# Head loads of a hybrid attention block: [hi; lo] keys, plain rows on SyncE's queue, 13 slots, five raw weight buffers

## The chip, the cores and the metric

One core of one Trainium2 chip runs the kernel. The metric is the device time of one execution in microseconds (us), as the median of several. The engines are TensorE (PE; its weight loads are listed as PEld), VectorE (DVE), ScalarE (ACT), GpSimd (POOL) and SyncE (SP). DMAs are issued by SyncE's and GpSimd's queues, each in its own order.

## The reference

One layer of a decoder over 1024 tokens of width 1024, in float32: a normalised input is projected once for three token mixers, their outputs are projected back and added, and a squared-ReLU MLP with a hidden width of 4096 follows.

```python
h = rms_norm(x, norm_mix[l])
proj = h @ w_in[l]
a_q, a_kv, a_g, b_qkv, c_qkv = jnp.split(proj, PROJ_SPLITS, axis=-1)
o_a = nsa_mixer(...)             # 4 heads: compressed, selected and window attention, gated
o_b = dilated_mixer(...)         # 3 groups (dilation 1, 4, 16) of 2 heads, merged by denominators
o_c = stick_breaking_mixer(...)  # 6 heads: sigmoid scores, running products from the right
cat = jnp.concatenate([...], axis=-1)
x = x + cat @ w_out[l]
h = rms_norm(x, norm_mlp[l])
x = x + jnp.square(jax.nn.relu(h @ w_up[l])) @ w_down[l]
```

Heads have 64 columns. All attention is causal, in blocks of 128 queries.

## The kernel before

Every float32 operand of a matmul is split into two float32r halves, hi (a rounded copy, on ScalarE) and lo (what is left, on VectorE or GpSimd); `put` (L107) does both. A dense product is three matmuls (hi·hi, hi·lo, lo·hi) that add up in one PSUM bank.

The tokens are two halves of 512. Queries and keys of the stick-breaking and dilated heads are projected pair by pair (two heads are 128 columns), split, and spilled to DRAM tensors `q_d`, `k_d` (`spill_qk`, L538): for each pair one store of the hi tile and one of the lo tile, each with 128 rows, the two heads' 64 columns one below the other. Values go to `v_d` with hi and lo side by side in the free dimension (`spill_v`). NSA queries of the second half go to `nq_d` in the same way (L443); those of the first half stay in SBUF.

A unit of attention work loads its heads with `load_heads` (L597). A key tile has the 64 hi rows above the 64 lo rows of one head. The query tiles `qh` and `ql` have the hi rows twice and the lo rows twice, so the two matmuls of `scores` (L632) give hi·hi + hi·lo and lo·hi + lo·lo. All these loads are issued by GpSimd: for a pair two of qh, two of ql, two of k, two of v; for a single head two of q, one of k, one of v; for NSA four. The q loads read their source rows twice, and the k loads step over the two stored parts with an outer dimension. v is read as it lies.

The tiles of these loads come from one pool of 11 slots of 128 x 1024 (`slots`, L119). The program that writes the kernel keeps a count of live slots (`live`, `take`, `free`, `prefetch`, L1322) against `SLOTS` (L213); a unit whose slots don't fit is loaded after another one has ended. Units need: stick-breaking pair 4 slots in the first half and 6 in the second, dilated unit 6 and 9, NSA 4 for keys and values and 2 for each pair of heads' queries. Probabilities lie in the `ck` pool (10 buffers).

Units run in the order: first half stick-breaking pairs 0, 1, 2, dilated 0, 1, NSA; second half NSA, stick-breaking 0, 1, dilated 0, 1, stick-breaking 2. While one unit's probabilities are multiplied with the values, the next one's scores are made (`both`, L1351); the dilated units of the second half run alone. Between the steps of the units the program puts steps of a filler: projections, then the output projection and the MLP of the first half. After the last unit the second half's output projection and MLP run without attention. Dilated units exchange softmax statistics through DRAM (`xch`, L951 to L966, SyncE).

Weights of the input projection are loaded by SyncE into raw buffers (`wraw`, two of them, L168) in parts of 128 x 512; `split` (L176) casts and subtracts a part and then asks for the part after next. A weight group has two or four parts; the next group is fetched as soon as a group comes into use (`next_w`, L316). Split weights lie in pairs of tiles `whi`, `wlo` (three pairs). Output and MLP weights go through `load_rows` (L1042): into the same raw buffers at first, and into four of their own once the MLP's pool is open.

The order of the instructions on each engine is set when the kernel is built, from the program above and a simulated timeline; each engine then works in that order.

Of the kernel before, what the change touches and what calls it, by code (L numbers as in the profile page):

```python
# [15 lines left out]

S, D, HD, DFF = 1024, 1024, 64, 4096
NB = S // 128
EPS = 1e-6
WMAX = 268  # L20
# [39 lines left out]
def tile_trunk(ctx, tc, x, xT, w_in, w_out, w_up, w_down, cw1, cw2, small, t_nsa, t_dil, out):  # L60
# [24 lines left out]
    r_d = dram.tile([S], F32, name="r_d")  # L85
    nq_d = dram.tile([2, 2, 2, 64, 512], F32, name="nq_d")
    q_r, k_r, v_r, nq_r = [t.bitcast(F32R) for t in (q_d, k_d, v_d, nq_d)]

# [29 lines left out]
    hctx = ExitStack()  # L118
    slots = actx.enter_context(tc.tile_pool(name="slots", bufs=11))  # L119
    ckp = actx.enter_context(tc.tile_pool(name="ck", bufs=10))  # L120
    ptp = actx.enter_context(tc.tile_pool(name="pT", bufs=3))
# [19 lines left out]
    def load_w(key):  # L141


        if key[0] == 'w1':
            n, pieces, src, o0 = 128, 2, cw1[key[1]], 0
        else:
            n = len(W_GROUPS[key])
            pieces, src, o0 = 1 if n == 128 else 2, w_in, W_OFF[key]
        res, parts = [], []
        k = 8 if key[0] == 'w1' else 8 // pieces  # L150
        for i in range(pieces):
            o = o0 + i * k * n
# [12 lines left out]
        def load(part):  # L165
            dst = part[1]
            m = dst.shape[1] * (dst.shape[2] if len(dst.shape) == 3 else 1)
            raw = wpool.tile([128, 2 * WMAX], F32, tag="wraw", bufs=2, name="wraw")[:, :m]  # L168
            i = nc.sync.dma_start(raw, src[:, part[0]:part[0] + m])
            if clock[0] < 10.0:  # L170
                in_order(i)
            return raw.rearrange("p (k c) -> p k c", c=128) if len(dst.shape) == 3 else raw

        raws = [load(p) for p in parts[:2]]

        def split():  # L176
            for i, (_, hi, lo) in enumerate(parts):
                put(hi, lo, raws[i], pool=i % 2 == 1 and len(w_keys) < 14)
                if i + 2 < len(parts):
                    raws.append(load(parts[i + 2]))  # L180
                if i % 2:
                    yield
        return res, split()
# [28 lines left out]
    FLIP, START, END = 1.3, 5.0, 2.5  # L212
    SLOTS = 11  # L213
    live = [2]
# [214 lines left out]
    def nsa_q(W_q, half):  # L429
# [6 lines left out]
        def fin(p):  # L436
            tp = pair_T(v2, 128 * p)
            if half == 1:
                hi, lo = [sg_t("tnq", F32R)[:, :512] for _ in range(2)]
                for i, r in ((0, A), (1, B)):  # L440
                    put(hi[r], lo[r], tp[r], qg[r, 2 * p + i:2 * p + i + 1])
                for part, t in enumerate((hi, lo)):
                    nc.sync.dma_start(nq_d[p, part].rearrange("h d t -> (h d) t"), t.bitcast(F32))  # L443
                return
            nsa['q', 0, p] = hi, lo = [slot(n).rearrange("p (h t) -> p h t", h=2) for n in ("nqh", "nql")]
            for i, r in ((0, A), (1, B)):
                put(hi[A, i], lo[A, i], tp[r], qg[r, 2 * p + i:2 * p + i + 1])
                nc.scalar.copy(hi[B, i], hi[A, i].bitcast(F32))
                nc.vector.tensor_copy(lo[B, i], lo[A, i].bitcast(F32))
        for p in range(2):  # L450
# [85 lines left out]


    def spill_qk(pair, j, cs, hi, lo):  # L538
        for part, t in enumerate((hi, lo)):
            nc.sync.dma_start((q_d, k_d)[j][pair, part, :, cs], t.bitcast(F32))  # L540

# [50 lines left out]

    def rows_of(t, *dims):

        return bass.AP(tensor=t.tensor, offset=t.offset, ap=[list(d) for d in dims])

    def load_heads(pair, half, heads=(0, 1)):  # L597

        q0, nk = 512 * half, 512 * (half + 1)
        ks = slice(0, nk)  # L600
        n = len(heads)
        hs = slice(heads[0], heads[0] + n)
        halves = lambda t: t.rearrange("p (h s) -> p h s", h=2)
        part, twice = (128 * S, 2), (0, 2)
        if n == 1:
            r = 64 * heads[0]
# [11 lines left out]
        qh, ql = [halves(slot(nm)) for nm in ("qh", "ql")]  # L618
        k, v = [[t[:, 0], t[:, 1]] if half == 0 else [t, slot(nm)]
                for nm in "kv" for t in [halves(slot(nm)) if half == 0 else slot(nm)]]  # L620
        for i, t in enumerate((qh, ql)):
            for h in heads:
                r = 64 * h
                nc.gpsimd.dma_start(t[:, h], rows_of(q_r[pair, i, r:r + 64, q0:q0 + 512], twice, (S, 64), (1, 512)))
        for h in heads:
            r = 64 * h
            nc.gpsimd.dma_start(k[h], rows_of(k_r[pair, 0, r:r + 64, ks], part, (S, 64), (1, nk)))
        for h in heads:
            nc.gpsimd.dma_start(v[h], v_r[pair, h, :, ks])
        return [(qh[:, h], ql[:, h], k[h], v[h]) for h in heads]  # L630

    def scores(qh, ql, n, k, masked=False):  # L632

# [4 lines left out]
        cs = slice(128 * n, 128 * n + 128)  # L638
        nc.tensor.matmul(o, qh[:, cs], k, start=True, stop=False)  # L639
        if masked:  # L640
            nc.tensor.matmul(o[:, w - 128:w], ident_r, ahead, start=False, stop=False)
        nc.tensor.matmul(o, ql[:, cs], k, start=False, stop=True)  # L642
        return ps
# [101 lines left out]
    class Nsa(Unit):  # L745
# [21 lines left out]
        def branch(self, i, chunks, kt, vt, gate, l0):  # L767

            n, h = self.n, 2 * self.hp + i
            (qh, ql), sl, st = [t[:, i] for t in nsa['q', self.half, self.hp]], SLOPES[6 + h], self.st[i]  # L770
            prev = None
            for k, (p, c0, tab) in enumerate(chunks):
                w = p.shape[-1]
                acc = st[:, 4 * l0 + k:4 * l0 + k + 1]
                ps = scores(qh, ql, n % 4, kt[:, c0:c0 + w])
                biased(ps, w, tab, sl, p, acc, prev)
# [55 lines left out]
    class Sb(Unit):  # L832
# [16 lines left out]
        def weights(self, n, c0):  # L849

            qh, ql, k, _ = self.head
# [4 lines left out]
            ps = scores(qh, ql, n % 4, k[:, c0:c0 + w], masked=after is None)  # L856
            nc.scalar.activation(b[:, :w], ps[:, :w], AF.Sigmoid, scale=-0.125)
# [37 lines left out]
    class Dil(Unit):  # L895
# [18 lines left out]
        def probs(self):  # L914
# [9 lines left out]
            for ro in range(4):  # L924
# [9 lines left out]
                for g in (1, 2):  # L934
                    qh, ql, k, _ = hd[g]
                    if half == 0:
# [4 lines left out]
                    acc = acc_t[:, ro:ro + 1] if g == 1 else stP[:, ro, 0:1]  # L941
                    biased(scores(qh, ql, ro, k), w, dtab[:, 256 * g - w:256 * g], 4.0 * sl[g], p, acc, prev)
                    prev = acc
# [8 lines left out]
            nc.sync.dma_start(self.oN, dP.rearrange(nat, p=128))  # L952
            qh, ql, k, _ = hd[0]
            for i in range(4):
# [5 lines left out]
                p = pn[-1][:, 256 * (i % 2):256 * (i % 2) + w]  # L960
                ps = scores(qh, ql, i, k[:, c0:c0 + w])
                biased(ps, w, dtab[:, 256 - w:256], sl[0], p, stN[:, i, 0:1], None)
# [74 lines left out]
    def raw_tile():  # L1037
        if 'mp' in late:
            return late['mp'].tile([128, 512], F32, tag="raw", bufs=4, name="raw")
        return wpool.tile([128, 2 * WMAX], F32, tag="wraw", bufs=2, name="wraw")[:, :512]  # L1040

# [419 lines left out]
```

## Time and profile before

| | us |
|---|---|
| median of 3 runs | 1473.87 (1472.23 to 1474.32) |
| the profiled execution | 1478.49 |
| span of its trace | 1476.7 |
| TensorE busy | 1347.3 |
| VectorE busy | 836.8 |
| GpSimd busy | 684.3 |
| ScalarE busy | 647.7 |

The span runs from the first to the last instruction of the profiled execution. Busy times are sums of an engine's instructions, without those that only issue DMAs or wait (GpSimd's DMA issues are counted). The granted clock of TensorE is a share of its full 2.4 GHz. "Idle before" an instruction is the time that its engine stood still just before it, with what ended that.

### The profile page before, as it was taken

Reading aid. Unit: us, or ns where it says so; the run is one execution under the profiler, and the core shown is the slowest. Engines: PE = TensorE matmul, PEld = TensorE weight load, DVE = VectorE, ACT = ScalarE, POOL = GpSimd, SP = SyncE. Lnnn points to the kernel's source line nnn. Section 1 sums busy time; section 2 is a strip of 40 time slices with the busy share of each in tenths; the row PEclk is TensorE's granted clock in tenths of the full one; section 3 lists DMA queues with packets and bytes.
Section 4 is the critical chain, followed back from the end, with each engine's and each line's share of the span. In section 5 each row is a group of like instructions: output and inputs, shape, how many; then the busy total and the mean of one; then the engine's idle time right before and its main releaser. Section 6 shows DMA issues by size and latency. Waiting matters only on the chain.

```text
span 1476.7 us, 21132 instructions
## 1 busy us (share of the span) xinstructions
PE 1347.3 (91%) x7241; PEld 1156.5 (78%) x7241; DVE 836.8 (57%) x1973; ACT 647.7 (44%) x1453; POOL 684.3 (46%) x614
## 2 busy tenths in 40 slices
PE   8887978688797999999997696999999999999998
PEld 6876978688786887888886585788888888888887
DVE  7365664468566998888885353783453332332333
ACT  6234554357454666555564142553343222222221
POOL 2123224434673424454556252534755555556553
PEclk9999989899798999999999798999999999999999
DMA  5697566852734422244548545224434333333332
GB/s 180 166 187 192 143 148 152 152 134 61 136 95 144 137 62 61 73 119 115 122 113 146 94 110 110 75 62 136 123 111 145 89 100 94 92 100 92 95 100 86
DMA packets 178572, 171.65 MB, mean 116 GB/s; under 512 B 89376, under 2 KB 105248, under 8 KB 178464
## 3 DMA queue, kind: packets, MB, share of 16 engines
q1 hardware_dynamic: 91808, 136.45, 32.5%
q0 software_dynamic: 86656, 33.85, 13.0%
q8 instruction: 57, 0.93, 0.3%
q14 instruction: 51, 0.42, 0.1%
HBM read 142.67 MB, written 27.30 MB: 115 GB/s over the span
## 4 chain that ended last, share of the span: by engine, by line
PE 67%; DMA 13%; DVE 11%; issue 4%; ACT 4%; SPq 1%; POOL 1%; DVEq 0%; ACTq 0%; POOLq 0%
PE pd L1094 25%; PE pd L1160 23%; DMA wraw<-in_w_in_dram 6%; PE pd L250 6%; PE ptp L684 3%; DMA k<-k_d 2%; PE pd L258 2%; PE po L705 2%; PE po L700 2%; PE pscore L642 1%; PE pscore L639 1%; DMA xch<-stx 1%; DMA wraw<-in_cmp_w_dram 1%; ACT whi L103 1%; DVE b L864 1%
## 5 line engine op out<-in xcount | busy, mean ns | idle before, releaser
L112 POOL TENSOR_TENSOR wlo<-raw,whi 128x512 fp32r<-128x512 f32 x264 | 351.1, 1350 | 370.9 <-ACT whi L103 365.6
L1094 PE MATMUL pd<-whi,hid 128*128 128x512 f32 x1120 | 381.6, 401 | 4.1 <-DVE acc L1099 2.6
L1099 DVE SCALAR_TENSOR_TENSOR acc<-pd,rs,acc 128x512 f32<-128x512 f32 x256 | 191.0, 747 | 117.5 <-PE pd L1094 116.6
L1094 PEld LDWEIGHTS pd<-whi,hid 128*128 128x128 f32 x1120 | 212.2, 189 | 51.9 <-DVE acc L1099 4.3
L103 ACT CAST whi<-raw 128x512 fp32r<-128x512 f32 x264 | 150.6, 619 | 180.7 <-issue 87.8
L1094 PE MATMUL pd<-wlo,hid 128*128 128x512 f32 x560 | 221.7, 396 | 0.0
L1160 PE MATMUL pd<-h_hi,whi 128*128 128x512 f32 x512 | 203.2, 397 | 0.2 <-ACT h_hi L105 0.2
L1160 PE MATMUL pd<-h_lo,whi 128*128 128x512 f32 x512 | 203.0, 398 | 0.0
L1160 PE MATMUL pd<-h_hi,wlo 128*128 128x512 f32 x512 | 202.3, 395 | 0.0
L1164 DVE TENSOR_TENSOR sqr<-sqr 128x512 f32<-128x512 f32 x64 | 49.4, 772 | 263.0 <-ACT sqr L1163 262.7
L250 PE MATMUL pd<-whi,hT_hi 128*128 128x256 f32 (+1 forms) x512 | 155.4, 307 | 15.7 <-DVE vs L114 7.4
L250 PE MATMUL pd<-wlo,hT_hi 128*128 128x256 f32 (+1 forms) x512 | 153.1, 300 | 1.4 <-DVE wlo L112 1.4
L250 PE MATMUL pd<-whi,hT_lo 128*128 128x256 f32 (+1 forms) x512 | 151.7, 298 | 0.0
L1163 ACT ACTIVATE sqr<-pd 128x512 f32<-128x512 f32 x64 | 38.2, 597 | 211.6 <-PE pd L1160 211.6
L1094 PEld LDWEIGHTS pd<-wlo,hid 128*128 128x128 f32 x560 | 106.3, 190 | 20.2
L250 PEld LDWEIGHTS pd<-whi,hT_hi 128*128 128x128 f32 x512 | 104.1, 204 | 17.3 <-DVE vs L114 8.0
L1160 PEld LDWEIGHTS pd<-h_hi,wlo 128*128 128x128 f32 x512 | 97.0, 190 | 22.5
L1160 PEld LDWEIGHTS pd<-h_hi,whi 128*128 128x128 f32 x512 | 97.1, 190 | 22.1 <-ACT h_hi L105 0.7
L1160 PEld LDWEIGHTS pd<-h_lo,whi 128*128 128x128 f32 x512 | 96.4, 189 | 21.3
L112 DVE TENSOR_TENSOR pTlo<-ptp,pThi 128x512 fp32r<-128x512 f32 (+2 forms) x160 | 101.1, 638 | 19.5 <-ACT pThi L103 18.5
L250 PEld LDWEIGHTS pd<-wlo,hT_hi 128*128 128x128 f32 x512 | 105.2, 206 | 1.6 <-DVE wlo L112 1.6
L250 PEld LDWEIGHTS pd<-whi,hT_lo 128*128 128x128 f32 x512 | 104.5, 204 | 0.0
(279 smaller groups left out, 2585.7 us busy)
## 6 DMA issues: line engine op xcount, KB each, us to landing
raw<-in_w_down_dram SPq DMA_DIRECT2D x128, 256.0 KB, 2.9
raw<-in_w_up_dram SPq DMA_DIRECT2D x124, 256.0 KB, 2.9
wraw<-in_w_in_dram SPq DMA_DIRECT2D x66, 256.0 KB, 3.0
k<-k_d POOLq DMA_DIRECT2D x12, 512.0 KB, 19.8
v<-v_d POOLq DMA_DIRECT2D x12, 512.0 KB, 16.1
qh<-q_d POOLq DMA_DIRECT2D x20, 256.0 KB, 11.4
ql<-q_d POOLq DMA_DIRECT2D x20, 256.0 KB, 13.0
v_d<-vs SPq DMA_DIRECT2D x32, 128.0 KB, 3.0
```

The lines of the kernel that those rows point to most:

```text
L103: nc.scalar.copy(dst, src)
L112: eng.tensor_tensor(dst_lo, src, dst_hi.bitcast(F32), op=OP.subtract)
L250: nc.tensor.matmul(ps[:, :n], tokens(a, d, tb), b, start=(d == 0 and j == 0), stop=(d == 7 and j == 2))
L258: nc.tensor.matmul(ps, a, b[half][:, d], start=(d == 0 and j == 0), stop=(d == 7 and j == 2))
L684: nc.tensor.transpose(tp[:, off:off + 128], a, ident)
L700: nc.tensor.matmul(po[:, o0:o0 + w], vst, hi[:, src:src + w], start=(e == 0), stop=False)
L705: nc.tensor.matmul(*rest, start=False, stop=last and s not in held)
L1094: nc.tensor.matmul(ps, a[:, cs], b, start=(k == 0), stop=(k == last))
L1099: nc.vector.scalar_tensor_tensor(acc[:, tb, os_], ps, r2[:, t:t + 1], acc[:, tb, os_], op0=OP.mult, op1=OP.add)
L1160: nc.tensor.matmul(ps, a[:, ds], b[:, d], start=(d == 0 and j == 0), stop=(d == 7 and j == 2))
L1163: nc.scalar.activation(h, ps, AF.Relu)
L1164: nc.vector.tensor_tensor(h, h, h, op=OP.mult)
```

## The change

`q_d`, `k_d` and `nq_d` now hold, for each head, 64 hi rows above 64 lo rows, and a spill is four stores of 64 rows instead of two of 128. Keys are then loaded as they lie. Queries become q1 = [hi; lo] and q2 = [lo; hi]: q1 is loaded as it lies, q2 in two loads of 64 rows. For a pair of heads q1 is one load of both heads, q2 two; k and v are one load each in the first half and two each in the second. The products of `scores` are the same four in other pairs (hi·hi + lo·lo, then lo·hi + hi·lo). All these loads are issued by SyncE. No DMA is issued by GpSimd, and the scratch for such DMAs is cut to 1024. The slot pool and its count go from 11 to 13, the `ck` pool from 10 to 11, the raw weight buffers from 2 to 5, and `load_w` asks for up to five parts at once. The NSA queries of the first half are put into the new order in SBUF with the same number of copies.

```diff
+SLOTS = 13
+RAWS = 5
...
-    nq_d = dram.tile([2, 2, 2, 64, 512], F32, name="nq_d")
-    q_r, k_r, v_r, nq_r = [t.bitcast(F32R) for t in (q_d, k_d, v_d, nq_d)]
+    nq_d = dram.tile([2, 2, 128, 512], F32, name="nq_d")
...
-    slots = actx.enter_context(tc.tile_pool(name="slots", bufs=11))
-    ckp = actx.enter_context(tc.tile_pool(name="ck", bufs=10))
+    slots = actx.enter_context(tc.tile_pool(name="slots", bufs=SLOTS))
+    ckp = actx.enter_context(tc.tile_pool(name="ck", bufs=11))
...
-            raw = wpool.tile([128, 2 * WMAX], F32, tag="wraw", bufs=2, name="wraw")[:, :m]
+            raw = wpool.tile([128, 2 * WMAX], F32, tag="wraw", bufs=RAWS, name="wraw")[:, :m]
...
-        raws = [load(p) for p in parts[:2]]
+        raws = [load(p) for p in parts[:RAWS]]
...
-                if i + 2 < len(parts):
-                    raws.append(load(parts[i + 2]))
+                if i + RAWS < len(parts):
+                    raws.append(load(parts[i + RAWS]))
...
-                for part, t in enumerate((hi, lo)):
-                    nc.sync.dma_start(nq_d[p, part].rearrange("h d t -> (h d) t"), t.bitcast(F32))
+                for rows, t in ((A, hi), (B, lo)):
+                    spill_rows(nq_d[p, 0, rows], 128 * 512, t)
                 return
-            nsa['q', 0, p] = hi, lo = [slot(n).rearrange("p (h t) -> p h t", h=2) for n in ("nqh", "nql")]
+            nsa['q', 0, p] = q1, q2 = [slot(n).rearrange("p (h t) -> p h t", h=2) for n in ("nq1", "nq2")]
             for i, r in ((0, A), (1, B)):
-                put(hi[A, i], lo[A, i], tp[r], qg[r, 2 * p + i:2 * p + i + 1])
-                nc.scalar.copy(hi[B, i], hi[A, i].bitcast(F32))
-                nc.vector.tensor_copy(lo[B, i], lo[A, i].bitcast(F32))
+                put(q1[A, i], q1[B, i], tp[r], qg[r, 2 * p + i:2 * p + i + 1])
+                nc.scalar.copy(q2[B, i], q1[A, i].bitcast(F32))
+                nc.vector.tensor_copy(q2[A, i], q1[B, i].bitcast(F32))
...
+    def spill_rows(dst, step, t):
+
+        for h, rows in ((0, A), (1, B)):
+            ap = bass.AP(tensor=dst.tensor, offset=dst.offset + h * step, ap=[list(e) for e in dst.ap])
+            nc.sync.dma_start(ap, t[rows].bitcast(F32))
+
     def spill_qk(pair, j, cs, hi, lo):
-        for part, t in enumerate((hi, lo)):
-            nc.sync.dma_start((q_d, k_d)[j][pair, part, :, cs], t.bitcast(F32))
+        for rows, t in ((A, hi), (B, lo)):
+            spill_rows((q_d, k_d)[j][pair, 0, rows, cs], 128 * S, t)
...
+    def fetch(t, src):
+        nc.sync.dma_start(t.bitcast(F32), src)
+
+    def fetch_q(q1, q2, src):
+
+        fetch(q1, src)
+        fetch(q2[A], src[B])
+        fetch(q2[B], src[A])
...
-            for i in range(2):
-                nc.gpsimd.dma_start(qq[:, i], rows_of(q_r[pair, i, r:r + 64, q0:q0 + 512], twice, (S, 64), (1, 512)))
+            fetch_q(qq[:, 0], qq[:, 1], q_d[pair, h, :, qs])
...
-            nc.gpsimd.dma_start(k, rows_of(k_r[pair, 0, r:r + 64, ks], part, (S, 64), (1, nk)))
-            nc.gpsimd.dma_start(v, v_r[pair, heads[0], :, ks])
+            fetch(k, k_d[pair, h, :, ks])
+            fetch(v, v_d[pair, h, :, ks])
...
+        q = [halves(slot(nm)) for nm in ("q1", "q2")]
+        fetch_q(*q, by_head(q_d[pair], qs))
+        kv = []
+        for nm, d in (("k", k_d), ("v", v_d)):
+            if half == 0:
+                t = halves(slot(nm))
+                fetch(t, by_head(d[pair], ks))
+                t = [t[:, 0], t[:, 1]]
+            else:
+                t = [slot(nm) for _ in heads]
+                for h in heads:
+                    fetch(t[h], d[pair, h, :, ks])
+            kv.append(t)
...
-                qs = nsa['q', 1, self.hp] = [slot(nm).rearrange("p (h t) -> p h t", h=2) for nm in ("nqh", "nql")]
-                for part, t in enumerate(qs):
-                    for i in range(2):
-                        nc.gpsimd.dma_start(t[:, i], rows_of(nq_r[self.hp, part, i], (0, 2), (512, 64), (1, 512)))
+                qs = nsa['q', 1, self.hp] = [slot(nm).rearrange("p (h t) -> p h t", h=2) for nm in ("nq1", "nq2")]
+                fetch_q(*qs, nq_d[self.hp].rearrange("h p t -> p h t"))
...
-    nc = _bacc.Bacc("TRN2", target_bir_lowering=False, num_devices=1)
+    nc = _bacc.Bacc("TRN2", target_bir_lowering=False, num_devices=1, dynamic_dma_scratch_size=1024)
```

## Rows read from the trace of the kernel before

**Rows 1.** The page, its first lines: span, then TensorE's busy time.

```profile
span 1476.7 us, 21132 instructions
...
PE 1347.3 (91%) x7241; PEld 1156.5 (78%) x7241; DVE 836.8 (57%) x1973; ACT 647.7 (44%) x1453; POOL 684.3 (46%) x614
```

**Rows 2.** Stretches: length, busy us of PE, PEld, DVE, ACT, POOL, clock, DMA share, GB/s.

```profile
50.00:500.00 450.00, 374.13 (x2516) 347.80 (x2517) 273.23 (x851) 219.13 (x571) 185.13 (x198) 0.89 0.61 147
500.00:800.00 300.00, 296.94 (x1642) 253.76 (x1641) 253.62 (x613) 177.48 (x411) 143.49 (x129) 1.00 0.39 97
800.00:910.00 110.00, 74.62 (x338) 61.93 (x337) 42.02 (x113) 29.08 (x66) 38.78 (x36) 0.81 0.65 116
910.00:1476.70 566.70, 559.87 (x2519) 457.16 (x2517) 239.28 (x343) 193.17 (x363) 306.57 (x236) 1.00 0.33 100
```

**Rows 3.** Stretches at clock 0.50, sums: fourteen in 50 to 500, three in 800 to 910.

```profile
sum 95.57, PE 66.05 PEld 63.21 DVE 55.00 ACT 41.96 POOL 30.45; mean PE 4.72 PEld 4.51 DVE 3.93 ACT 3.00 POOL 2.17
...
sum 40.95, PE 17.46 PEld 14.95 DVE 2.80 ACT 0.92 POOL 0.93; mean PE 5.82 PEld 4.98 DVE 0.93 ACT 0.31 POOL 0.31
```

**Rows 4.** Timeline of TensorE: start, duration, instruction, idle before and its end.

```profile
91.52 0.45 PE L639 MATMUL pscore<-k,qh 128*128 128x128 f32 x1 [5.48 <-DMA k<-k_d]
...
820.48 0.55 PE L639 MATMUL pscore<-k,qh 128*128 128x256 f32 x1 [16.92 <-issue]
...
823.44 0.55 PE L639 MATMUL pscore<-k,qh 128*128 128x256 f32 x1 [2.19 <-issue]
...
899.22 0.45 PE L639 MATMUL pscore<-k,qh 128*128 128x128 f32 x1 [13.30 <-DMA k<-k_d]
```

**Rows 5.** Lines L629 (v, issued at 630.1) and L627 (k, at 796.4): landing.

```profile
DMA to landing us min/median/max: 3.6/3.6/3.6
...
DMA to landing us min/median/max: 24.0/24.0/24.0
```

**Rows 6.** The page, DMA issues: queue, count, KB each, median us to landing.

```profile
wraw<-in_w_in_dram SPq DMA_DIRECT2D x66, 256.0 KB, 3.0
k<-k_d POOLq DMA_DIRECT2D x12, 512.0 KB, 19.8
...
acc<-in_x_dram SPq DMA_DIRECT2D x8, 512.0 KB, 6.9
```

**Rows 7.** The page, DMA queues: packets, MB, share of 16 engines' time.

```profile
q1 hardware_dynamic: 91808, 136.45, 32.5%
q0 software_dynamic: 86656, 33.85, 13.0%
```

**Rows 8.** The page, the chain that ended last, by line.

```profile
PE pd L1094 25%; PE pd L1160 23%; DMA wraw<-in_w_in_dram 6%; PE pd L250 6%; PE ptp L684 3%; DMA k<-k_d 2%; PE pd L258 2%; PE po L705 2%; PE po L700 2%; PE pscore L642 1%; PE pscore L639 1%; DMA xch<-stx 1%; DMA wraw<-in_cmp_w_dram 1%; ACT whi L103 1%; DVE b L864 1%
```

**Rows 9.** The chain in order of time, 274 to 296: start, us, what.

```profile
274.24 9.33 DMA wraw<-in_w_in_dram
283.67 0.65 ACT whi L103
284.34 0.73 DVE wlo L112
285.08 10.10 DMA wraw<-in_w_in_dram
```

**Rows 10.** Stretches of 50 us in stage A, columns as in rows 2.

```profile
150.00:200.00 50.00, 48.76 (x389) 48.27 (x389) 31.90 (x72) 26.18 (x67) 19.45 (x18) 0.94 0.60 147
...
400.00:450.00 50.00, 46.87 (x354) 43.62 (x353) 35.04 (x135) 27.43 (x77) 33.30 (x37) 0.97 0.41 109
```

**Rows 11.** Timeline of SyncE: start, duration, twelve stores issued in a row.

```profile
217.48 8.42 SPq L572 DMA_DIRECT2D v_d<-vs  x12
```

**Rows 12.** Waits of SyncE's queue: us in total, times, longest.

```profile
SPq L1045 <- POOL wlo L112: 650.1, 258, 15.9
```

**Rows 13.** Groups of GpSimd by line: busy, mean ns, idle before, releasers.

```profile
L627 POOL DMA_DIRECT2D k<-k_d x20 | 16.3, 833 | 24.1 <-DMA k_d<-tlo 13.1 <-PE pscore L642 10.9
L629 POOL DMA_DIRECT2D v<-v_d x20 | 12.2, 632 | 25.0 <-DMA v_d<-vs 15.6 <-PE pscore L642 5.9 <-PE po L705 3.5
```

More of the change, by code (lines that the diff above doesn't have):

```diff
@@ L212, in tile_trunk @@
     FLIP, START, END = 1.3, 5.0, 2.5
-    SLOTS = 11
     live = [2]
@@ L590, in spill_dqk @@
             later(6.0, lambda j=j, g=g: fin(j, g))
-    def rows_of(t, *dims):
-        return bass.AP(tensor=t.tensor, offset=t.offset, ap=[list(d) for d in dims])
+    def fetch(t, src):
[4 more added lines that the diff above has]
+        fetch(q2[B], src[A])
     def load_heads(pair, half, heads=(0, 1)):
[L599 to L602, printed above, removed]
+        qs, ks = slice(512 * half, 512 * half + 512), slice(0, 512 * half + 512)
         halves = lambda t: t.rearrange("p (h s) -> p h s", h=2)
-        part, twice = (128 * S, 2), (0, 2)
-        if n == 1:
-            r = 64 * heads[0]
+        by_head = lambda d, cs: d[:, :, cs].rearrange("h p s -> p h s")
+        if len(heads) == 1:
+            h = heads[0]
             qq = halves(slot("qq"))
-            for i in range(2):
-                nc.gpsimd.dma_start(qq[:, i], rows_of(q_r[pair, i, r:r + 64, q0:q0 + 512], twice, (S, 64), (1, 512)))
+            fetch_q(qq[:, 0], qq[:, 1], q_d[pair, h, :, qs])
             if half == 0:
@@ L614, in load_heads, with scores @@
                 k, v = slot("k"), slot("v")
-            nc.gpsimd.dma_start(k, rows_of(k_r[pair, 0, r:r + 64, ks], part, (S, 64), (1, nk)))
-            nc.gpsimd.dma_start(v, v_r[pair, heads[0], :, ks])
+            fetch(k, k_d[pair, h, :, ks])
+            fetch(v, v_d[pair, h, :, ks])
             return [(qq[:, 0], qq[:, 1], k, v)]
[L618 to L632, printed above, removed]
+        q = [halves(slot(nm)) for nm in ("q1", "q2")]
[11 more added lines that the diff above has]
+            kv.append(t)
+        return [(q[0][:, h], q[1][:, h], kv[0][h], kv[1][h]) for h in heads]
+    def scores(q1, q2, n, k, masked=False):
         ps = ps_s()
@@ L638, in scores @@
         cs = slice(128 * n, 128 * n + 128)
-        nc.tensor.matmul(o, qh[:, cs], k, start=True, stop=False)
+        nc.tensor.matmul(o, q1[:, cs], k, start=True, stop=False)
         if masked:
             nc.tensor.matmul(o[:, w - 128:w], ident_r, ahead, start=False, stop=False)
-        nc.tensor.matmul(o, ql[:, cs], k, start=False, stop=True)
+        nc.tensor.matmul(o, q2[:, cs], k, start=False, stop=True)
         return ps
@@ L769, in branch @@
             n, h = self.n, 2 * self.hp + i
-            (qh, ql), sl, st = [t[:, i] for t in nsa['q', self.half, self.hp]], SLOPES[6 + h], self.st[i]
+            (q1, q2), sl, st = [t[:, i] for t in nsa['q', self.half, self.hp]], SLOPES[6 + h], self.st[i]
             prev = None
@@ L774, in branch @@
                 acc = st[:, 4 * l0 + k:4 * l0 + k + 1]
-                ps = scores(qh, ql, n % 4, kt[:, c0:c0 + w])
+                ps = scores(q1, q2, n % 4, kt[:, c0:c0 + w])
                 biased(ps, w, tab, sl, p, acc, prev)
@@ L849, in weights @@
         def weights(self, n, c0):
-            qh, ql, k, _ = self.head
+            q1, q2, k, _ = self.head
             Wn = 128 * (n + 1)
@@ L855, in weights @@
             after = self.after.get(n)
-            ps = scores(qh, ql, n % 4, k[:, c0:c0 + w], masked=after is None)
+            ps = scores(q1, q2, n % 4, k[:, c0:c0 + w], masked=after is None)
             nc.scalar.activation(b[:, :w], ps[:, :w], AF.Sigmoid, scale=-0.125)
@@ L934, in probs @@
                 for g in (1, 2):
-                    qh, ql, k, _ = hd[g]
+                    q1, q2, k, _ = hd[g]
                     if half == 0:
@@ L941, in probs @@
                     acc = acc_t[:, ro:ro + 1] if g == 1 else stP[:, ro, 0:1]
-                    biased(scores(qh, ql, ro, k), w, dtab[:, 256 * g - w:256 * g], 4.0 * sl[g], p, acc, prev)
+                    biased(scores(q1, q2, ro, k), w, dtab[:, 256 * g - w:256 * g], 4.0 * sl[g], p, acc, prev)
                     prev = acc
@@ L952, in probs @@
             nc.sync.dma_start(self.oN, dP.rearrange(nat, p=128))
-            qh, ql, k, _ = hd[0]
+            q1, q2, k, _ = hd[0]
             for i in range(4):
@@ L960, in probs @@
                 p = pn[-1][:, 256 * (i % 2):256 * (i % 2) + w]
-                ps = scores(qh, ql, i, k[:, c0:c0 + w])
+                ps = scores(q1, q2, i, k[:, c0:c0 + w])
                 biased(ps, w, dtab[:, 256 - w:256], sl[0], p, stN[:, i, 0:1], None)
@@ L1039, in raw_tile @@
             return late['mp'].tile([128, 512], F32, tag="raw", bufs=4, name="raw")
-        return wpool.tile([128, 2 * WMAX], F32, tag="wraw", bufs=2, name="wraw")[:, :512]
+        return wpool.tile([128, 2 * WMAX], F32, tag="wraw", bufs=RAWS, name="wraw")[:, :512]
     def load_rows(src, hi, lo):
```

## The prediction, made before the changed kernel ran

> **What bounds the kernel now.** I read the page first, then the stretches by stage, the chain of waits, the waits of TensorE, the landing times of the DMAs, and last the waits of GpSimd's and SyncE's queues. TensorE is the bound: busy 1347.3 of 1476.7 us [rows 1]. So the change can only win what TensorE now loses, in two ways: idle time, and work done at the lower of its two clock levels (1.2 instead of 2.4 GHz, granted clock 0.50). The stages show where [rows 2]. From 500 to 800 and from 910 to the end TensorE is idle for 3.1 and 6.8 us at a granted clock of 1.00; nothing is to be had there. From 50 to 500 (projections, spills, first attention units) it is idle for 450 - 374.1 = 75.9 us at a mean clock of 0.89. From 800 to 910 (second half of the dilated units, then the last stick-breaking pair) it is idle for 110 - 74.6 = 35.4 us at 0.81. The sums over the stretches at clock 0.50 hold 66.05 and 17.46 us of TensorE work [rows 3], half of which, 33.0 and 8.7 us, goes back if the clock stays up; all of them follow or hold idle time. What is lost: stage A (50 to 500) 109 us, stage B (800 to 910) 44 us.
>
> What TensorE waits for in B is plain: idle for 16.92 and 13.30 us before score products, the second released by a landing of k; in A, 5.48 us before the first score product, also k [rows 4]. (The first is put down to "issue", but its k was requested at 796.4 and took 24.0 us to land, to 820.4, as TensorE starts [rows 4, 5].) The landing times say why. k loads of 512 KB on GpSimd's queue take 19.8 us in the median; SyncE's 512 KB loads of x, four issued together, 6.9 us, and its 256 KB weight loads 3.0 us [rows 6]. A v load of the same 512 KB, on the same GpSimd queue, alone, lands in 3.6 us [rows 5]. v's rows are read plainly; k and q come from a source with an outer step over parts or heads, the q rows twice. The queues tell the difference: the software queue moved 33.85 MB in 86656 packets, 390 bytes each, SyncE's 136.45 MB in 91808, 1486 bytes each [rows 7]. So I read the slowness as one of the pattern and of GpSimd's queue, and it hits others: in A the chain runs through weight loads (6% of the span over all [rows 8]), of which two in a row took 9.33 and 10.10 us beside a burst of head loads, against that 3.0 us. In between stand a cast and a subtraction that give the raw buffer back [rows 9]: with two raw buffers the next load is asked for only then, so each latency goes into the chain.
>
> **The change part by part.**
> *Rows and queue of the loads.* The 104 head loads on GpSimd become 86 on SyncE (ten pairs: five or seven each; four singles of five; two NSA groups of three), of the same bytes, in plain rows. A k load is then third or fourth in its group; nearest row, the burst of x loads: 6.9 us for 512 KB. I take 8 us; bounds are 3.6 us (a plain row alone) and 24.0 us (no better). Stage B: k asked for at 796.4 lands at 804.4, when TensorE wants it at 803.6 (820.48 - 16.92). With the 2.19 us before the second product [rows 4], some 19.1 us of waiting shrink to 3: 16 back. The last pair's k, asked for at 879.7 with a landing of 19.4 us, comes at 887.7 instead of 899.1, wanted at 885.9: 11.6 of 13.3 back. That is 27.6 of 35.4 idle us, and in proportion 0.78 x 8.7 = 6.8 of clock: 34 us, between 0 and 44.
> The Trainium skill speaks against this gain. "Trainium Kernel Development and Optimization" (Key Constraints) says that DMAs issued from SP, ACT and POOL run on the same 16 engines and interleave, so that another issuing queue saves its issue time alone; "DMA: Bandwidth & Descriptors" (Anatomy of one DMA, SWDGE path) gives 2.0 us plus bytes over 436 GB/s for a GpSimd DMA, an estimated 3.2 us for 512 KB. The v load alone agrees (3.6 us); k at 24.0 us doesn't. By these pages the sum would be that of rival 1.
> *Five raw buffers.* No weight group has more than four parts, so all of them are requested when the group is, and neither cast nor subtraction stands between two loads. With the shorter head loads this is stage A's gain. Upper bound: its best slices, of which the first and the last of three stand [rows 10], lose 1.2, 3.8 and 3.1 us to idleness and (50 us times one minus the clock of 0.94, 0.94, 0.97) 3.0, 3.0 and 1.5 us to the clock, 5.2 in the mean; nine such slices lose 47 of 109, so at most 62 comes back. Lower bound 5, the one k wait. Two thirds of a hindered weight load (9.33 against 3.0 us) is hindrance; I take two thirds of 62: 40 us. Next late there are ScalarE's in-order work and score banks, not removed.
> *13 slots, 11 ck buffers.* Both dilated units of the first half (6 + 6 slots) now fit at once, and a second-half stick-breaking pair beside NSA's six or beside another pair; two dilated units of the second half (9 + 9) still don't. I count nothing of its own: where it helps it is inside A's or B's bound. It can cost something if earlier loads go ahead of weights, which is in the SyncE term.
> *Stores per head.* 48 spills become 96 and 4 NSA spills 8, half the rows each: 52 more issues. With 86 loads SyncE issues 138 DMAs more. Its row price is 0.70 us an issue in a packed run of 12 stores [rows 11]: 97 us at most of its time, over 1477 us. SyncE stands waiting for raw buffers for 650.1 us in L1045 alone [rows 12], so the issues are hidden; where stores come packed, before 500 us, they may delay a weight load by a few us. If that cover were gone, they would cost up to those 97.
> *Waits that move to SyncE.* GpSimd now stands idle before head loads for 90.2 us in eight groups, of which the two largest stand (49.1 us) [rows 13]: for a spill to land, or for TensorE to release a slot. On SyncE the same waits hold back whatever is queued behind, that is weight loads, spills and the softmax exchange of the dilated units; ScalarE's casts wait for those, then TensorE. Bounds 0 and 90 on the path. Five raw buffers before 500 us and four raw plus three split pairs later are cover for most; I take 15. GpSimd loses its issue time and these waits; busy for 185 of 450 and 39 of 110 us in the two stages [rows 2], it is off the path.
> *No cost:* the new order of hi and lo in q1 and q2 leaves the products and copies the same in number and size, and the first 50 us issue no head load.
>
> **The sum.** 40 + 34 - 15 = 59 us off the profiled execution's 1478.5 us gives 1419.5. That execution lies 4.6 us above the median of the three, 1473.87; on their scale I predict 1415 us.
>
> **The rivals.**
> 1. *The head loads become no faster*: the DMA engines or the bytes limit them. For it: the bytes stay, and the loads of a group still come in one burst. Against it: the lone v load and the packet sizes. Then B gives 5 us (earlier requests through two more slots) and A half of 40: 25 - 15 = 10, so 1464 us.
> 2. *SyncE's order eats part of it*: half of the 90 us of waits is exposed: 74 - 45 = 29, so 1445 us. For it: SyncE already waits in almost every L1045 load, and a head load stands in the same line. Against it: each single wait is a few us, and buffers lie ahead.
> 3. *Slower*: all of those waits reach TensorE, because in A a head load that waits for its spill holds the next group's weights just as that group is wanted: 74 - 90 = -16, so 1490 us. It turns slower once over 74 of the 90 us are exposed. Against it: the weights of a group are asked for before the loads of a unit that needs its spill.
> 4. *More than forecast*: both bounds are reached and SyncE costs nothing: 62 + 44 = 106, so 1368 us. For it: nothing else is late in B. Against it: A has other waits, on ScalarE and VectorE.
>
> **Chances and range.** Forecast (1390 to 1435) 0.52, rival 1 0.14, rival 2 0.14, rival 3 0.12, rival 4 0.08. A measurement of this kernel can tell about 0.2% (3 us) from no change. Within that I put 0.02 of rival 1 and 0.01 each of 2 and 3: faster 0.85, same 0.04, slower 0.11. The range from 1382 to 1464 leaves out rival 3, a few hundredths of rival 1 and about half of rival 4, 0.2 in all.
>
> **What would show it.** Right: no software queue among the DMA queues, and some 80 thousand packets fewer; head loads from SyncE that land in 3 to 9 us; no TensorE wait above 5 us before a score product after 800 us; weight loads well under 6% of the chain; a granted clock over stage A above 0.92 against 0.89. Wrong by rival 1: head loads still over 12 us. By rivals 2 and 3: SyncE waiting for a spill or for TensorE in the head loads, and behind it ScalarE's casts waiting for weights. The forecast falls if stage A keeps its 76 us of idleness though its weight loads have become short.

## The result and the profile after

The changed kernel takes 1370.64 us in the median, against 1473.05 for the kernel before: a ratio of 0.9317 (95% interval 0.9281 to 0.9353), 102 us less. The forecast was 1415, with a range that began at 1382: the direction was right, the size was not, and the time came out where rival 4 had it (1368). The profiled execution took 1368.75 us.

The page of the changed kernel: span, busy times, the one queue that is left, the chain by line.

```profile
span 1366.8 us, 21134 instructions
...
PE 1321.6 (97%) x7241; PEld 1133.8 (83%) x7241; DVE 846.1 (62%) x1973; ACT 646.8 (47%) x1453; POOL 610.7 (45%) x510
...
q1 hardware_dynamic: 107328, 170.01, 42.7%
...
PE pd L1100 27%; PE pd L1166 24%; PE pd L250 8%; PE ptp L692 3%; PE pd L258 3%; PE po L713 2%; PE po L708 2%; DMA xch<-stx 2%; PE pscore L650 2%; PE pscore L647 2%; DVE pTlo L113 1%; DMA xr<-in_xT_dram 1%; DVE acc L1108 1%; DMA r_d<-rs 1%; DVE psel L655 1%
```

TensorE is busy for 97% of the span instead of 91% [rows 1]. The software queue is gone [rows 7]; what moves is the same 170 MB. Loads of weights, 6% of the chain before [rows 8], no longer stand among its first entries.

The page, DMA issues: queue, count, KB each, median us to landing.

```profile
wraw<-in_w_in_dram SPq DMA_DIRECT2D x66, 256.0 KB, 3.9
k<-k_d SPq DMA_DIRECT2D x17, 512.0 KB, 4.6
v<-v_d SPq DMA_DIRECT2D x17, 512.0 KB, 5.5
q<-q_d SPq DMA_DIRECT2D x10, 512.0 KB, 5.4
```

A k load lands in 4.6 us instead of 19.8 [rows 6]. To see where the time went, the span is cut where TensorE has started the same numbers of matmuls as at 50, 500, 800 and 910 us of the kernel before. The stretches of the changed kernel, columns as in rows 2:

```profile
0.00:57.30 57.30, 42.70 (x233) 36.01 (x233) 28.77 (x57) 29.47 (x46) 8.91 (x17) 0.95 0.54 166
57.30:426.60 369.30, 353.91 (x2516) 331.79 (x2517) 282.59 (x852) 218.22 (x574) 142.75 (x137) 0.96 0.64 176
426.60:731.10 304.50, 302.33 (x1642) 257.18 (x1641) 252.07 (x605) 177.40 (x405) 126.73 (x103) 1.00 0.32 97
731.10:800.80 69.70, 64.90 (x337) 54.20 (x336) 36.19 (x79) 26.87 (x56) 28.62 (x23) 0.98 0.47 138
800.80:1366.80 566.00, 557.76 (x2519) 454.59 (x2518) 246.48 (x382) 194.85 (x374) 303.67 (x233) 1.00 0.34 102
```

The kernel before, cut at the same counts (in it the 233rd matmul waits until 54.6), in stages A and B:

```profile
54.60:500.10 445.50, 374.18 (x2516) 347.81 (x2517) 272.17 (x850) 218.77 (x571) 185.23 (x198) 0.89 0.61 146
...
800.10:910.20 110.10, 74.72 (x337) 62.01 (x336) 42.12 (x114) 29.28 (x66) 38.69 (x36) 0.81 0.65 115
```

Stage A became 445.5 - 369.3 = 76.2 us shorter, stage B 110.1 - 69.7 = 40.4. The first stretch got 2.7 us longer, the middle 4.5 longer, the last 0.5 shorter: 109.9 us in all, the difference of the two spans. (The medians differ by 102, because the profiled execution before lies 4.6 us above its median and the one after 1.9 below.) In stage A TensorE is idle for 15.4 us instead of 71.3, at a clock of 0.96 instead of 0.89; in B for 4.8 instead of 35.4, at 0.98 instead of 0.81.

TensorE's waits in the changed kernel: what for, us in total, times, longest. Then SyncE's two largest waits at the head loads (L600).

```profile
PE pd L258 <- ACT hT_hi L106: 9.6, 3, 5.8
PE ptp L692 <- DVE p L663: 5.3, 3, 2.7
PE pd L250 <- DVE vs L115: 5.0, 1, 5.0
```

```profile
SPq L600 <- PE pscore L650: 22.8, 11, 5.0
SPq L600 <- PE po L713: 18.4, 5, 7.1
```

No wait for k is left among TensorE's largest, and none over 5.8 us, where there were 16.92 and 13.30 [rows 4]. SyncE does stand at the head loads, for TensorE to give slots back, up to 7.1 us at a time; TensorE's list shows nobody who pays for it.

### The profile page after: what moved, and what is told of

The parts are those of the page before. It is cut to its first block, busy times and chain, and to the rows that moved or that the text cites. A ratio compares the mean times of both kernels' runs of the same rounds, so it can differ in the third digit from the quotient of the medians.

```text
span 1366.8 us, 21134 instructions
## 1 busy us (share of the span) xinstructions
PE 1321.6 (97%) x7241; PEld 1133.8 (83%) x7241; DVE 846.1 (62%) x1973; ACT 646.8 (47%) x1453; POOL 610.7 (45%) x510
## 2 busy tenths in 40 slices
DMA packets 107435, 171.36 MB, mean 125 GB/s; under 512 B 18240, under 2 KB 34112, under 8 KB 107328
## 3 DMA queue, kind: packets, MB, share of 16 engines
q1 hardware_dynamic: 107328, 170.01, 42.7%
## 4 chain that ended last, share of the span: by engine, by line
PE 76%; DVE 11%; DMA 7%; issue 3%; ACT 2%; SPq 1%; POOL 1%; DVEq 0%; ACTq 0%; POOLq 0%
PE pd L1100 27%; PE pd L1166 24%; PE pd L250 8%; PE ptp L692 3%; PE pd L258 3%; PE po L713 2%; PE po L708 2%; DMA xch<-stx 2%; PE pscore L650 2%; PE pscore L647 2%; DVE pTlo L113 1%; DMA xr<-in_xT_dram 1%; DVE acc L1108 1%; DMA r_d<-rs 1%; DVE psel L655 1%
## 5 line engine op out<-in xcount | busy, mean ns | idle before, releaser
L113 POOL TENSOR_TENSOR wlo<-raw,whi 128x512 fp32r<-128x512 f32 x264 | 355.1, 1366 | 413.5 <-ACT whi L104 400.3
L250 PE MATMUL pd<-whi,hT_hi 128*128 128x256 f32 (+1 forms) x512 | 149.3, 293 | 6.7 <-DVE vs L115 5.0
L250 PE MATMUL pd<-wlo,hT_hi 128*128 128x256 f32 (+1 forms) x512 | 147.1, 288 | 1.6 <-DVE wlo L113 1.6
L250 PE MATMUL pd<-whi,hT_lo 128*128 128x256 f32 (+1 forms) x512 | 146.4, 287 | 0.0
L104 ACT CAST pThi<-ptp 128x512 fp32r<-128x512 f32 (+2 forms) x160 | 86.5, 551 | 48.9 <-PE ptp L692 45.5
L250 PEld LDWEIGHTS pd<-whi,hT_hi 128*128 128x128 f32 x512 | 98.0, 192 | 8.1 <-DVE vs L115 5.2
L113 POOL TENSOR_TENSOR wlo<-wraw,whi 128x512 fp32r<-128x512 f32 (+1 forms) x42 | 58.3, 1394 | 98.6 <-ACT whi L104 67.9
```

The costliest lines, as they stand in the source:

```text
L104: nc.scalar.copy(dst, src)
L113: eng.tensor_tensor(dst_lo, src, dst_hi.bitcast(F32), op=OP.subtract)
L250: nc.tensor.matmul(ps[:, :n], tokens(a, d, tb), b, start=(d == 0 and j == 0), stop=(d == 7 and j == 2))
```

## The experiments

Three questions: which part of the change carries the gain; whether the old head loads were slow through GpSimd's queue or through the way in which their reads were described; and whether SyncE's order cost what the forecast took for it.

**Only layout, stores and loads** (slots and buffers as before):

```diff
-SLOTS = 13
-RAWS = 5
+SLOTS = 11
+RAWS = 2
...
-    ckp = actx.enter_context(tc.tile_pool(name="ck", bufs=11))
+    ckp = actx.enter_context(tc.tile_pool(name="ck", bufs=10))
```

> The changed kernel with 11 slots, 10 ck buffers and two raw weight buffers, as before: only layout, stores and loads are changed. Theory P (the stepped reads make the head loads slow, and slow loads hold up every other transfer): most of the 102 us gain is here, 1395 to 1415 us, and TensorE idles for under 60 us. Theory B (the raw buffers and slots carry the gain up to 500 us, the loads only that from 800 to 910): 1435 to 1450 us, weight loads still 4% or more of the chain.

1390.21 us, ratio 0.9447 (0.9419 to 0.9475): 81 of the 102 us. Stages A and B:

```profile
53.70:441.60 387.90, 360.63 (x2516) 336.37 (x2517) 270.44 (x846) 216.73 (x569) 138.69 (x136) 0.94 0.60 166
...
741.40:815.20 73.80, 69.81 (x338) 57.83 (x336) 32.10 (x74) 26.92 (x55) 33.03 (x26) 0.98 0.43 129
```

The loads alone bring 445.5 - 387.9 = 57.6 us of stage A and 36.3 of B. The time is 5 us under theory P's range, and TensorE idles for 61 us (1390.8 - 1329.7) where P said under 60; theory B's 1435 to 1450 us is excluded.

**The same plain loads on GpSimd's queue:**

```diff
     def fetch(t, src):
-        nc.sync.dma_start(t.bitcast(F32), src)
+        nc.gpsimd.dma_start(t.bitcast(F32), src)
```

> As e1_loads_only, but the head loads, in their new plain rows, are issued by GpSimd with the default scratch. Theory P (pattern): k of 512 KB lands in 4 to 8 us, the time is within 15 us of e1_loads_only. Theory Q (GpSimd's queue is slow or its waits hold up its subtractions): k lands in over 10 us and the time is 1440 us or more.

1391.92 us, ratio 0.9458 (0.9432 to 0.9483): no difference from SyncE's queue over the whole kernel that these runs can tell. (Within the profiled executions stage A is 9.5 us longer than on SyncE, 397.4 against 387.9, and the stretches after it together that much shorter.) From its DMA view:

```profile
q0 software_dynamic: 9568, 33.56, 7.9%
...
k<-k_d POOLq DMA_DIRECT2D x17, 512.0 KB, 5.9
```

GpSimd's own queue lands a 512 KB k load in 5.9 us, and needs 9568 packets for the 33.6 MB instead of 86656 [rows 7]. The queue itself was not what made the old loads slow. Theory Q falls.

**The old, stepped reads on SyncE's queue** (the kernel before, all seven kinds of head load alike):

```diff
-            nc.gpsimd.dma_start(k, rows_of(k_r[pair, 0, r:r + 64, ks], part, (S, 64), (1, nk)))
+            nc.sync.dma_start(k.bitcast(F32), rows_of(k_d[pair, 0, r:r + 64, ks], part, (S, 64), (1, nk)))
...
-                nc.gpsimd.dma_start(t[:, h], rows_of(q_r[pair, i, r:r + 64, q0:q0 + 512], twice, (S, 64), (1, 512)))
+                nc.sync.dma_start(t[:, h].bitcast(F32), rows_of(q_d[pair, i, r:r + 64, q0:q0 + 512], twice, (S, 64), (1, 512)))
```

> The kernel before with its stepped and doubled reads, issued by SyncE instead of GpSimd, all else as before. Theory P: the loads stay slow, k in 10 us or more, and the time is 1440 us or more. Theory Q: k lands in 4 to 8 us, the time is within 15 us of e1_loads_only.

1691.52 us, ratio 1.1501 (1.147 to 1.1531): 221 us slower than the kernel before. The timeline of SyncE's queue in the first burst, and three stretches of 5 us in it (length, busy times, clock, DMA share, GB/s):

```profile
73.45 10.69 SPq L624 DMA_DIRECT2D ql<-q_d  x2
84.18 10.34 SPq L627 DMA_DIRECT2D k<-k_d  x2
94.57 5.70 SPq L629 DMA_DIRECT2D v<-v_d  x2
100.37 1.28 SPq L169 DMA_DIRECT2D wraw<-in_w_in_dram  x2
```

```profile
84.00:89.00 5.00, 0.05 (x1) 0.00 (x0) 4.16 (x8) 3.04 (x4) 1.20 (x1) 0.99 0.13 50
89.00:94.00 5.00, 0.00 (x0) 0.00 (x0) 0.00 (x0) 0.00 (x0) 0.29 (x1) 0.50 0.13 50
94.00:99.00 5.00, 0.00 (x0) 0.00 (x0) 0.00 (x0) 0.00 (x0) 0.00 (x0) 0.50 0.13 50
```

With four to six loads issued, the sixteen DMA engines are busy for 0.13 of their time and move 50 GB/s. Two sixteenths are 0.125, so the share reads as two engines at work and fourteen idle; the trace's packet records agree, with two packets under way at once for 91% of these 15 us and never more than three, where the changed kernel has sixteen or more while a pair's heads are loaded (85 to 90 us). SyncE itself hangs in the issue of two loads for over 10 us, where two weight loads a little later took 1.28 us, and whatever is queued behind them waits. (This trace has no landing times; TensorE waits for k up to 19.9 us at a time.) The packet count (105771) is as low as in the changed kernel (107435), so small packets, on which the prediction leaned, are not what makes these loads slow. This gave theory E: an outer dimension of two steps spreads a load over two DMA engines only.

**Only five raw buffers** (the kernel before; the scratch made smaller to fit them):

```diff
-            raw = wpool.tile([128, 2 * WMAX], F32, tag="wraw", bufs=2, name="wraw")[:, :m]
+            raw = wpool.tile([128, 2 * WMAX], F32, tag="wraw", bufs=5, name="wraw")[:, :m]
...
-        raws = [load(p) for p in parts[:2]]
+        raws = [load(p) for p in parts[:5]]
...
-                if i + 2 < len(parts):
-                    raws.append(load(parts[i + 2]))
+                if i + 5 < len(parts):
+                    raws.append(load(parts[i + 5]))
...
-    nc = _bacc.Bacc("TRN2", target_bir_lowering=False, num_devices=1)
+    nc = _bacc.Bacc("TRN2", target_bir_lowering=False, num_devices=1, dynamic_dma_scratch_size=11264)
```

> The kernel before with five raw weight buffers instead of two (the scratch of GpSimd's DMAs goes to 11264 bytes to make room), all else as before. Theory B: 1425 to 1440 us, weight loads leave the chain. Theory P: 1450 to 1470 us, the head loads stay at 17 to 20 us for 512 KB and TensorE still waits for k by 13 us and more after 800 us.

1436.53 us, ratio 0.9761 (0.973 to 0.9791). Stages A and B, two of TensorE's waits after 760 us, and from the page the loads' landing:

```profile
59.40:463.70 404.30, 361.77 (x2517) 338.69 (x2518) 278.69 (x851) 218.35 (x572) 190.52 (x200) 0.94 0.66 160
...
763.70:872.20 108.50, 72.50 (x337) 60.19 (x336) 43.69 (x116) 29.30 (x66) 39.10 (x36) 0.83 0.66 117
```

```profile
783.72 0.55 PE L639 MATMUL pscore<-k,qh 128*128 128x256 f32 x1 [16.63 <-issue]
...
860.98 0.45 PE L639 MATMUL pscore<-k,qh 128*128 128x128 f32 x1 [13.58 <-DMA k<-k_d]
```

```profile
wraw<-in_w_in_dram SPq DMA_DIRECT2D x66, 256.0 KB, 5.9
k<-k_d POOLq DMA_DIRECT2D x12, 512.0 KB, 20.2
```

Both theories were half right. Stage A gives 41.2 us though weight loads land later than before (5.9 against 3.0 us [rows 6]): they are asked for early, and they have left the first entries of the chain; one of 9.49 us still stands in it, at 215.8. Stage B is as it was, with its two waits for k. In stage A the two parts of the change overlap: loads alone 57.6, buffers alone 41.2, together 76.2.

**The stepped loads split in two** (the kernel before, layout and stores kept; each load of two steps becomes two loads of 64 plain rows, on SyncE):

```diff
+    def fetch(t, src):
+        nc.sync.dma_start(t.bitcast(F32), src)
+
+    def fetch2(t, a, b):
+        fetch(t[A], a)
+        fetch(t[B], b)
...
-            nc.gpsimd.dma_start(k[h], rows_of(k_r[pair, 0, r:r + 64, ks], part, (S, 64), (1, nk)))
+            fetch2(k[h], k_d[pair, 0, r:r + 64, ks], k_d[pair, 1, r:r + 64, ks])
```

> The kernel before, loads on SyncE as in e8_steps_on_sync, but each read with an outer step of two is split into two loads of 64 plain rows (184 head loads instead of 104); layout, stores, slots and raw buffers as before. Theory E (a load whose outermost dimension has two steps is spread over two of the sixteen DMA engines): 1385 to 1410 us, no stretch of waiting at a DMA share of 0.13, issues of loads under 1 us. Theory L (it is the distance between the parts, or reading rows twice, that is slow): over 1440 us, as slow loads as in e8.

1377.78 us, ratio 0.9345 (0.9316 to 0.9374). Stages A and B:

```profile
54.10:428.90 374.80, 350.34 (x2516) 327.82 (x2517) 266.79 (x851) 218.00 (x571) 141.59 (x137) 0.97 0.58 172
...
727.70:803.20 75.50, 68.35 (x338) 56.61 (x337) 34.86 (x91) 27.81 (x62) 28.39 (x22) 0.95 0.57 154
```

The time is 7 us under theory E's range. Against the stepped loads on the same queue the split alone brings 314 us. Rows are still read twice and the parts still lie apart, so theory L falls.

**The same split on GpSimd's queue:** `nc.gpsimd` in place of `nc.sync` in `fetch`.

> As e9_split_steps, but the split loads stay on GpSimd's queue: the kernel before with nothing but its stepped loads split. Theory E: 1385 to 1415 us (80 more issues on GpSimd of some 0.6 us may cost up to 15), packets of the software queue near 10 to 15 thousand instead of 86656. Theory L: over 1440 us.

1404.81 us, ratio 0.9525 (0.9495 to 0.9554). The software queue took 11136 packets. So the kernel before, with nothing but its stepped loads cut in two, is 69 us faster. With 184 loads instead of 86 the queue does matter: 27 us more than on SyncE, all of it in stage A (404.9 against 374.8).

**The number of steps varied** (the changed kernel, its k loaded head by head in 24 loads, described with two steps of 64 rows or four of 32, each step beginning one row early so that the steps stay apart; so one or three rows of each key tile are read twice and as many last rows left out. v is loaded head by head too):

```diff
+    def fetch_k(t, src):
+        (s, _), (e, n) = list(src.ap)
+        nc.sync.dma_start(t.bitcast(F32), bass.AP(tensor=src.tensor, offset=src.offset, ap=[[63 * s, 2], [s, 64], [e, n]]))
...
-            fetch(k, k_d[pair, h, :, ks])
+            fetch_k(k, k_d[pair, h, :, ks])
```

> The changed kernel, but each of the 24 k loads is described with an outer dimension of two steps of 64 rows, 63 rows apart (so one row is read twice and the last one left out; k and v are loaded head by head in the first half too). Bytes, packets and queue are those of plain loads. Theory E (the number of outer steps sets how many of the sixteen DMA engines take part): a 512 KB k load goes at some 50 GB/s, over 10 us; while TensorE waits for one alone the DMA share is 0.13; time 1400 us or more. Theory L (rows read twice or far apart): as the changed kernel, 1365 to 1380 us.

> As e12_k_steps2 with four steps of 32 rows, 31 rows apart (three rows are read twice and the last three left out). Theory E: four engines, some 100 GB/s, DMA share 0.25 where a k load runs alone; time between the changed kernel and e12_k_steps2, 1375 to 1400 us. Theory L: as e12_k_steps2 whichever way that goes.

With two steps 1443.97 us (ratio 0.9826, 0.9768 to 0.9883), with four 1404.95 (0.956, 0.9503 to 0.9618), and 1370.64 without. A stretch of each, with two steps one in which TensorE waits and 512 KB loads alone are under way, with four one in which parts of weight loads run beside the k loads:

```profile
802.00:806.00 4.00, 0.29 (x1) 0.32 (x2) 0.00 (x0) 0.00 (x0) 0.00 (x0) 0.51 0.13 50
```

```profile
678.00:682.00 4.00, 4.00 (x19) 3.23 (x18) 0.72 (x3) 1.14 (x3) 0.45 (x1) 1.00 0.26 101
```

Two steps: a share of 0.13 and 50 GB/s. Four: 0.26 and 101. The packet records show two packets under way at once for 95% of the first stretch, four for 84% of the second. Between these two kernels bytes, queue and number of loads are the same, so the steps set the rate. The counts of packets on SyncE's queue, from the two pages, say the same:

```profile
q1 hardware_dynamic: 107152, 170.01, 40.6%
```

```profile
q1 hardware_dynamic: 107200, 170.01, 42.9%
```

In the changed kernel a plain head load makes 16 packets beyond its rows: 107328 less the 91808 of before and 52 x 16 for the added stores are 14688, which is 104 x 128 rows and 86 x 16. With ten more loads its 107328 packets would be 107488. Two steps leave 336 fewer, 14 for each of the 24 k loads; four steps 288 fewer, 12 for each. So 2 and 4 packets are left of the 16, which fits one for each engine that takes part. Four steps still cost 34 us, more than the forecast of up to 30.

**The changed kernel with two raw buffers** (`RAWS = 2`), **and with 11 slots and 10 ck buffers:**

> The changed kernel with two raw weight buffers instead of five. If the raw buffers carry what the loads alone leave (1390 against 1371 us): 1383 to 1390 us. If the slots carry it: 1370 to 1375 us.

> The changed kernel with 11 slots and 10 ck buffers instead of 13 and 11. If the raw buffers carry what the loads alone leave: 1370 to 1376 us. If the slots carry it: 1383 to 1390 us.

1384.64 us (ratio 0.9385, 0.9357 to 0.9413) and 1376.53 (0.9327, 0.9297 to 0.9357). Without the raw buffers stage A takes 387.6 us, with them and 11 slots 367.9: on top of the loads the raw buffers are worth 18 us of stage A, the slots nothing there. In stage B 11 slots take 75.0 us against 69.7, and with two raw buffers 73.8 against 69.6: the two slots and the ck buffer are worth 4 to 5 us of B. Over the whole kernel these two runs can't be told apart (0.9327 and 0.9317).

**More of the same:** the split loads in the old layout with all other parts of the change; eight raw buffers in place of the two slots (`SLOTS = 11`, `RAWS = 8`).

> e9_split_steps (old layout, stepped loads split, on SyncE) with the change's other parts: 13 slots, 11 ck buffers, five raw buffers. If the [hi; lo] layout and the stores per head are worth something of their own, 1372 to 1382 us, above the changed kernel's 1371; if they are not (the split alone is what they brought, and 48 store issues less count), 1358 to 1371 us.

> The changed kernel with 11 slots and eight raw buffers, in the space of the two slots. If weight loads still wait for a buffer: 1362 to 1370 us. If five are enough (no weight group has more than four parts): 1373 to 1379 us, as e6_slots11.

1369.31 us (ratio 0.931, 0.9284 to 0.9337) and 1375.19 (0.9352, 0.9327 to 0.9378). The first equals the changed kernel: the [hi; lo] layout and the stores per head bring nothing beyond doing away with the steps. The second shows that five buffers are enough.

**The start.** Runs with five raw buffers reach the 233rd matmul later (55.0 to 59.4) than those with two (53.4 to 54.6). These two kernels ask for two parts ahead in the first steps only, the second on top of the split loads:

```diff
-        raws = [load(p) for p in parts[:RAWS]]
+        ahead = 2 if clock[0] < 10.0 else RAWS
+        raws = [load(p) for p in parts[:ahead]]
```

> The changed kernel, but a weight group that is fetched in the first steps asks for two parts ahead, as before, instead of five; all later groups ask for five. If the first 50 us got longer because weight loads stand ahead of the x loads in SyncE's order: the 233rd matmul starts near 54 us instead of 57.3, and the time falls by 2 to 7 us, to 1364 to 1369. If it is the 13 slots or chance: no change, 1369 to 1373 us.

> e10_split_all with the same start. If the start's order costs: 1362 to 1367 us; else 1367 to 1371 us.

1371.01 us (0.9301, 0.9276 to 0.9326) and 1370.69 (0.929, 0.9264 to 0.9317), and the 233rd matmul still starts at 57.9 and 58.8. Neither start nor time changed: the guess about the order of weight and x loads is not borne out, and the cause of these few us stays open.

Stages A and B, cut at the same counts:

| kernel | median us | stage A | stage B |
|---|---|---|---|
| before | 1473 | 445.5 | 110.1 |
| changed | 1370.6 | 369.3 | 69.7 |
| loads only | 1390.2 | 387.9 | 73.8 |
| loads only, on GpSimd | 1391.9 | 397.4 | 72.8 |
| raw buffers only | 1436.5 | 404.3 | 108.5 |
| old reads on SyncE | 1691.5 | 571.9 | 106.6 |
| old reads split, SyncE | 1377.8 | 374.8 | 75.5 |
| old reads split, GpSimd | 1404.8 | 404.9 | 74.9 |
| changed, two raw buffers | 1384.6 | 387.6 | 69.6 |
| changed, 11 slots | 1376.5 | 367.9 | 75.0 |
| old reads split, all else changed | 1369.3 | 364.7 | 71.9 |
| changed, k in two steps | 1444.0 | 408.4 | 87.0 |
| changed, k in four steps | 1405.0 | 383.1 | 86.7 |

## Why the prediction was right in its direction and wrong in its size

*The bound and where the loss was: right.* Stages A and B held 109 and 44 us of loss, and all of the gain is there; 500 to 800 and the last 567 us moved by 4.5 and 0.5 us.

*Stage B, 34 us forecast, 40.4 measured: right, by the named waits.* k was taken to land in 8 us and landed in 4.6, so the waits of 16.92 and 13.30 us went wholly. The lone v load of 3.6 us [rows 5] was the nearer row, not the burst of x loads. With 11 slots B became 35 to 36 us shorter (75.0 and 73.8 us), close to the forecast; the 4 to 5 us more came with the slots, for which the prediction counted nothing.

*Stage A, 40 us forecast, 76.2 measured: the term that failed.* Its upper bound of 62 us took the best slices [rows 10] as what the stage could become, and two thirds of that as what it would. The bound was too low twice over. It counted nine such slices, the stage's old length; but the stage's work, 374 - 33 = 341 us at the upper clock, at 50 - 5.2 = 44.8 us a slice, fills 7.6 of them, so that the same rows gave a bound of 450 - 381 = 69 us. And the cured stage is better than those slices, which were made with two raw buffers, and in two of which (150 to 200 and 400 to 450) stepped loads were issued; that this is why they were worse is argued, not shown. After the change the stage loses 15.4 us to idleness and 369.3 x 0.04 = 14.8 to the clock, 30 us, where nine best slices had put 47 at least and the forecast 69. A safe bound comes from what TensorE's work needs, those 341 us; the stage now takes 369. With the full 76 in place of 40 the sum gives 1379.

*SyncE, 15 us forecast: nothing measured.* Same loads, same buffers, SyncE or GpSimd: 1390.2 and 1391.9 us, and with more loads SyncE is 27 us better. Without this term as well the sum is 1364, and with the 7 us that the first and middle stretches lost and the 6 us more of B, 1365 against 1371; the rest is where the two profiled executions lie against their medians. Waits did move to SyncE (22.8 and 18.4 us above), and buffers lay ahead of them, as the prediction said before it charged for them all the same.

*The cause: half right.* "The pattern and GpSimd's queue" was what the rows were read as; it was the pattern alone. The prediction saw that a plain v load on the same queue took 3.6 us and could have stopped there. It then took the packets for the sign of the pattern. They are a sign, but of another thing: the trace records 73344 of the 86656 packets with 4 bytes each, the rest being the 104 x 128 rows. That number is 80 stepped loads times 14 engines times 64, plus 104 times 16. That fits two engines with 64 rows each and 64 tiny packets on each of the other fourteen; this sharing out is arithmetic on totals, while 0.13 and 0.26 of the engines are measured. Whether those packets cost time of their own on GpSimd's queue no run shows, since the split took them away with the steps.

The Trainium skill has the rule, and the prediction missed it: "DMA: Bandwidth & Descriptors" (Why a DMA increments its semaphore by 16 and not by 1) says that a DMA is spread over the largest number of engines up to 16 that divides the slowest dimension of both sides. The traces agree: steps of 2 and 4 gave shares of 0.13 and 0.26.

*Rivals.* Rival 1 (loads no faster) falls with the landings of 4.6 us. Rivals 2 and 3 (SyncE's order) fall for this change. A neighbour of theirs is real: the old reads on SyncE's queue cost 221 us, and SyncE's queue is 8% of the chain there instead of 1%. But the rivals had waits for a spill or a slot in mind (8.3 and 6.9 us at the longest in that run), and there the issue of two stepped loads itself held the queue for over 10 us. Rival 4 held, though for another reason than its own: not because both bounds were reached but because the bound on A was too low. It had 0.08, and the range cut through it.

## What to carry to other kernels

Look at a DMA's outermost dimension before looking at its queue: here a load described with two outer steps ran on two of sixteen DMA engines, at 50 GB/s, and cutting all 80 such loads in two plain ones was worth 69 us of 1473 without any other change. The DMA share and the GB/s of a stretch in which such transfers are alone show it at once (0.13 at 50 GB/s). And the best stretch of a hindered stage is no bound for what the stage becomes when it is cured (62 us here, 76 measured); take the bound from the work itself.

## What the runs showed of the hardware that was not expected

- The rate of the loads went with the number of their outer steps: 50 GB/s for two, 101 for four, with two and four packets under way at once.
- The issue itself can block: two stepped loads held SyncE's queue for 10.69 us, against 1.28 us for two weight loads in the same burst. On GpSimd's queue the same loads were issued in some 0.8 us each, and the kernel was 221 us faster.
- Plain loads land nearly alike from either queue (512 KB of k, with the same buffers, in 5.0 us from SyncE's and 5.9 from GpSimd's).
- Not settled: why the split loads in the old layout (1377.8 us) do better than the whole ones in the new (1390.2) when both have two raw buffers, 374.8 against 387.9 us in stage A; with five buffers the two are equal.
